# Two of four weight-block sums formed by accumulating DMAs, with the gate paired with minus the up projection

## The chip, the cores and the metric

The kernel runs on one core of one Trainium2 chip. The metric is the time of one execution on the device in microseconds (us); the time before is the median of three runs. The profile comes from one more execution, which the hardware profiler recorded.

## The reference

One decoder layer on a sequence of 512 tokens with 1024 channels, in float32. Around a token mixer (two attention branches) stand two SwiGLU blocks; the change is in these alone:

```
x = x + 0.5 * swiglu(rms_norm(x, ffn1_norm), w_gate, w_up, w_down)
...                                   # two attention branches, gated and merged
x = x + 0.5 * swiglu(rms_norm(x, ffn2_norm), w_gate, w_up, w_down)
out = rms_norm(x, final_norm)

swiglu(x) = (silu(x @ w_gate) * (x @ w_up)) @ w_down     # w_gate, w_up 1024 x 2816, w_down 2816 x 1024
```

## The kernel before, in words

All matrix products are made of three passes: each operand is split into a high part (a cast to float32r) and a low part (the rest), and low times high, high times high and high times low are summed in PSUM. A weight split is two instructions: `split` (L105) lets ScalarE (ACT) cast (L109) and VectorE (DVE) subtract (L110), into three rotating buffers `whi` and `wlo`.

The 2816 hidden columns of a SwiGLU are worked off in 11 pairs of 256 columns by `ffn_up` (L454). The first two pairs (`PLAIN`, L452) are plain products, and during the second of these the scaled activations `xhat` and the operands of the fast scheme are built: `Operands.early` (L372) forms the sums T3, T2 and T4 of activation blocks and splits them into `t3h`, `t3l` and so on, `Operands.late` (L385) splits the four blocks B11, T1, B21 and B22 over the plain operand's place. The other nine pairs go through `strassen_pair` (L389), a two-by-two block scheme with seven products instead of eight. One product (L397) is 24 matmuls of 128x128 weights by 256 tokens: gate and up, four blocks of rows, three passes. In the kernel before, the two block rows of the weights are the two halves of the pair's columns, for gate and up at once; the two block columns are the even and odd row blocks. The DVE forms four sums of weight blocks of 128x1024 elements per pair: `s1` (L418, for the product with T1), `s2` (L420, for T2), the difference of L429 (for T3) and that of L433 (for B22). The products run in this order: B11, T1, T2, B21, T3, B22, T4. The bank `a` collects B11, T2, T3 and T4; ACT copies it to SBUF in between (`keep`, L408), and the DVE adds these copies to the banks `c` and `b` (L428, L432, L435) into `C`. SiLU, the product of gate and up, and the split of the result (`hidden`, L337) end the pair.

After every second fast pair a down projection of the two pairs before it follows (`down1`, L537; `down2`, L1126). The weights of a pair (2 MB) come by two loads on SP's queue (`load_pair`, L445) into one of two large buffers, `raw` and `fraw`, which pairs and down projections take in turn. SP's loads wait there for a buffer.

In the first SwiGLU, before pairs 4 to 8, `rope_table` (L509) forms a table of sines: POOL's queue loads the positions (L515), DVE and ACT work on them, POOL's queue stores the table (L529). Later POOL builds the causal mask (L589, L590).

The order in which each engine and each queue takes its instructions is worked out when the program is built: the framework places each instruction by its place in the code and by a model of when its operands are ready, and puts in the semaphores. On the chip every engine and every queue then works in that fixed order. Only the very beginning (up to L311) is ordered by hand.

`sums` is a pool of two buffers with one tag, which the temporaries of `early` use first and then `s1` and `s2` of each pair.

Of the kernel before, what the change touches and what calls it, by code (L numbers as in the profile page):

```python
# [8 lines left out]
F32 = mybir.dt.float32  # L9
F32R = mybir.dt.float32r  # L10
I32 = mybir.dt.int32
AF = mybir.ActivationFunctionType
ALU = mybir.AluOpType
AX = mybir.AxisListType

P = 128
T = 512
NB = T // P
DM = 1024
KT = DM // P  # L20
# [36 lines left out]
def hybrid_layer_kernel(ctx: ExitStack, tc: tile.TileContext, x, positions,  # L57
# [6 lines left out]
    nc = tc.nc  # L64
    vec, act, pool, pe = nc.vector, nc.scalar, nc.gpsimd, nc.tensor
# [39 lines left out]
    def split(src, eng=None):  # L105
        shape = list(src.shape)
        hi = wspl.tile(shape, F32R, name="whi", tag="whi")
        lo = wspl.tile(shape, F32R, name="wlo", tag="wlo")
        act.copy(hi, src)  # L109
        (eng or vec).tensor_tensor(out=lo, in0=src, in1=as_f32(hi), op=ALU.subtract)  # L110
        return hi, lo

    def kview(w, c0, c1):
        return w[0].rearrange("(a p) n -> p a n", p=P)[:, :, c0:c1]
# [88 lines left out]
    ffn1_stack = ExitStack()  # L203
# [17 lines left out]
        vec.tensor_copy(Rb, ps)  # L221


    def ffn_pools(stack):
        names = (("work", 1), ("tt", 1), ("sums", 2))
        return [stack.enter_context(tc.tile_pool(name=n, bufs=b)) for n, b in names]

    raws.append(ffn1_stack.enter_context(tc.tile_pool(name="fraw", bufs=1)).tile([P, RAW], F32, name="fraw"))
    ffn1_pools = ffn_pools(ffn1_stack)

    with tc.tile_pool(name="xnat", bufs=1) as xnp:
        xn = xnp.tile([P, NB, DM], F32, name="xn")
# [13 lines left out]
        with tc.manual_schedule(engines={EN.PE, EN.Activation, EN.DVE}):  # L246
# [57 lines left out]
            for tb in range(NB):  # L304
# [3 lines left out]
                else:  # L308
                    vec.tensor_tensor_reduce(out=junk, in0=xn[:, tb, :], in1=xn[:, tb, :], scale=1.0, scalar=0.0,
                                             op0=ALU.mult, op1=ALU.add, accum_out=ssq[:, tb:tb + 1])  # L310
# [16 lines left out]
    HT = T // 2  # L327
# [3 lines left out]
    def bank8():  # L331
        return bank(next(turn8))

    def halves(ps):
        return ps.rearrange("p (g t) -> p g t", g=2)
# [22 lines left out]
    class Operands:  # L358
# [11 lines left out]
            vec.tensor_tensor(out=lo, in0=src, in1=as_f32(hi), op=ALU.subtract)  # L370

        def early(self):  # L372
            B, new = self.B, lambda nm: self.sums.tile([P, KT // 2, HT], F32, name=nm, tag="S")
            t3 = new("sum_t3")
            vec.tensor_tensor(out=t3, in0=B[1][1], in1=B[0][1], op=ALU.subtract)
            vec.tensor_tensor(out=B[0][1], in0=B[0][1], in1=B[0][0], op=ALU.subtract)
            self.put("T3", t3)
            t2 = new("sum_t2")
            vec.tensor_tensor(out=t2, in0=B[1][1], in1=B[0][1], op=ALU.subtract)
            self.put("T2", t2)  # L380
            t4 = new("sum_t4")
            vec.tensor_tensor(out=t4, in0=B[1][0], in1=t2, op=ALU.subtract)
            self.put("T4", t4)

        def late(self):  # L385
            for name, (i, j) in (("B11", (0, 0)), ("T1", (0, 1)), ("B21", (1, 0)), ("B22", (1, 1))):
                self.put(name, self.B[i][j])

    def strassen_pair(work, sums, ops, raw, G):  # L389

        A = [[raw[:, :, j::2, (1 - i) * P:(2 - i) * P] for j in range(2)] for i in range(2)]
        shape = [P, 2, KT // 2, P]

        def new(nm):
            return sums.tile(shape, F32, name=nm, tag="S")

        def product(ps, w, t, first):  # L397
            (wh, wl), (th, tl) = w, ops.t[t]
            for g in range(2):
                o = ps[:, g * HT:(g + 1) * HT]  # L400
                for k in range(KT // 2):
                    n = g == 0 and k == 0
                    last = g == 1 and k == KT // 2 - 1
                    pe.matmul(o, wl[:, g, k, :], th[:, k, :], start=first and n, stop=False, skip_group_check=True)  # L404
                    pe.matmul(o, wh[:, g, k, :], th[:, k, :], start=False, stop=False, skip_group_check=True)  # L405
                    pe.matmul(o, wh[:, g, k, :], tl[:, k, :], start=False, stop=last, skip_group_check=True)  # L406

        def keep(ps, nm):  # L408
            t = work.tile([P, T], F32, name=nm, tag="w", bufs=6)
            act.copy(t, ps)  # L410
            return t

        C = work.tile([P, 3, T], F32, name="C")
        a = bank8()
        product(a, split(A[0][0]), "B11", True)
        p1 = keep(a, "p1")
        s1 = new("s1")
        vec.tensor_tensor(out=s1, in0=A[1][0], in1=A[1][1], op=ALU.add)  # L418
        s2 = new("s2")
        vec.tensor_tensor(out=s2, in0=s1, in1=A[0][0], op=ALU.subtract)  # L420
        c = bank8()
        product(c, split(s1), "T1", True)
        p5 = keep(c, "p5")
        product(a, split(s2), "T2", False)
        u2 = keep(a, "u2")
        b = bank8()
        product(b, split(A[0][1]), "B21", True)
        vec.tensor_tensor(out=C[:, 1, :], in0=b, in1=p1, op=ALU.add)  # L428
        vec.tensor_tensor(out=A[1][0], in0=A[0][0], in1=A[1][0], op=ALU.subtract)  # L429
        product(a, split(A[1][0]), "T3", False)  # L430
        u3 = keep(a, "u3")
        vec.tensor_tensor(out=C[:, 0, :], in0=u3, in1=p5, op=ALU.add)  # L432
        vec.tensor_tensor(out=A[0][0], in0=A[0][1], in1=s2, op=ALU.subtract)  # L433
        product(c, split(A[0][0]), "B22", False)
        vec.tensor_tensor(out=C[:, 2, :], in0=c, in1=u2, op=ALU.add)  # L435
        product(a, split(A[1][1]), "T4", False)
        av = halves(a)
        act.activation(G[:, 1:4, :], C[:, :, 0:HT], AF.Silu)
        act.activation(G[:, 0, :], av[:, 0, :], AF.Silu)
        vec.scalar_tensor_tensor(out=G[:, 1:4, :], in0=G[:, 1:4, :], scalar=0.5, in1=C[:, :, HT:T],  # L440
                                 op0=ALU.mult, op1=ALU.mult)
        vec.scalar_tensor_tensor(out=G[:, 0, :], in0=G[:, 0, :], scalar=0.5, in1=av[:, 1, :],
                                 op0=ALU.mult, op1=ALU.mult)

    def load_pair(w_gate, w_up, m):  # L445
        raw = space(2 * KT, 2 * P).rearrange("p (g k) c -> p g k c", g=2)
        for g, w in enumerate((w_gate, w_up)):
            nc.sync.dma_start(out=raw[:, g], in_=kview(w, 2 * m * P, (2 * m + 2) * P))
        return raw

    NPAIR = FT // 2
    PLAIN = 2  # L452

    def ffn_up(pools, hp, w_gate, w_up, X, xsrc, xhat, gname, r, first, extra, down):  # L454
        work, ttp, sums = pools
        xg = x_parts(X)
        hs = {}
        ops = None
        for m in range(PLAIN):
            G = new_G(work)  # L460
            raw = None
            for s in range(2):
                f = 2 * m + s
# [7 lines left out]
                else:  # L471
                    if raw is None:
                        raw = load_pair(w_gate, w_up, m)
# [10 lines left out]
                if m == PLAIN - 1 and s == 0:  # L484
# [3 lines left out]
                    ops = Operands(ttp, sums, X, xhat)  # L488
# [3 lines left out]
        for m in range(PLAIN, NPAIR):  # L492
            if extra is not None:
                extra(m)
            G = new_G(work)
            strassen_pair(work, sums, ops, load_pair(w_gate, w_up, m), G)
            hs[m] = hidden(work, hp, G)
            if m % 2 == 0 and m + 2 < NPAIR:
                down([(n, hs.pop(n)) for n in (m - 2, m - 1)])
# [3 lines left out]
    rc = const.tile([P, 20], F32, name="rc")  # L503
    pool.dma_start(out=rc, in_=rope_const)
    tabd = [dram.tile([P, T], F32, name=f"tabd{j}") for j in range(5)]
    wk1, ttp1, sums1 = ffn1_pools


    def rope_table(m):  # L509
# [757 lines left out]
```

## Time and profile before

| what | value |
|---|---|
| median of the runs | 1098.73 us (1096.1 to 1101.28) |
| profiled execution | 1097.36 us |
| its span | 1095.4 us |
| mean granted clock of the TensorE | 0.995 |
| PE, DVE, ACT, POOL busy | 98%, 74%, 47%, 5% |
| moved by DMA | 132.90 MB, 121 GB/s on the mean |

The profile counts an engine as busy while an instruction runs on it. PE is the TensorE's matmul, PEld its weight load, which overlaps the matmuls. Times are counted from the start of the span. "x24" stands for 24 instructions; in an order of time, the brackets at the end of a row give the time for which the engine stood idle before and what ended that. Clock 1.00 is 2.4 GHz.

### The profile page before, as it was taken

Reading aid. Unit: us, or ns where it says so; the run is one execution under the profiler, and the core shown is the slowest. Engines: PE = TensorE matmul, PEld = TensorE weight load, DVE = VectorE, ACT = ScalarE, POOL = GpSimd, SP = SyncE. Lnnn points to the kernel's source line nnn. Section 1 sums busy time; section 2 is a strip of 40 time slices with the busy share of each in tenths; the row PEclk is TensorE's granted clock in tenths of the full one; section 3 lists DMA queues with packets and bytes.
Section 4 is the critical chain, followed back from the end, with each engine's and each line's share of the span. In section 5 each row is a group of like instructions: output and inputs, shape, how many; then the busy total and the mean of one; then the engine's idle time right before and its main releaser. Section 6 shows DMA issues by size and latency. Waiting matters only on the chain.

```text
span 1095.4 us, 15774 instructions
## 1 busy us (share of the span) xinstructions
PE 1072.3 (98%) x6268; PEld 936.7 (86%) x6268; DVE 815.4 (74%) x1331; ACT 513.8 (47%) x828; POOL 52.2 (5%) x53
## 2 busy tenths in 40 slices
PE   8979999999999999999999999999999999999997
PEld 6778999999898888788877777788889999898995
DVE  5978787988766767998478776659777766767753
ACT  6453544535254434676365543444434435253544
POOL 1020000000000100122000000000000000000003
PEclk9999999999999999999999999999999999999999
DMA  9205253334315315442756358412242314225211
GB/s 289 96 4 161 78 169 121 106 107 158 93 58 159 121 49 153 111 139 78 242 168 222 109 165 290 150 44 73 77 154 78 116 39 153 78 77 154 77 59 77
DMA packets 107033, 132.90 MB, mean 121 GB/s; under 512 B 4070, under 2 KB 87184, under 8 KB 106960
## 3 DMA queue, kind: packets, MB, share of 16 engines
q1 hardware_dynamic: 97392, 111.32, 32.1%
q10 hardware_dynamic: 7664, 15.18, 4.2%
q0 software_dynamic: 1904, 5.40, 1.7%
q8 instruction: 49, 0.80, 0.3%
q14 instruction: 24, 0.20, 0.1%
HBM read 114.32 MB, written 17.04 MB: 120 GB/s over the span
## 4 chain that ended last, share of the span: by engine, by line
PE 92%; DVE 4%; DMA 2%; ACT 1%; issue 1%; SPq 0%; DVEq 0%; ACTq 0%
PE bank_gb L117 9%; PE bank_gb L119 8%; PE bank_gb L118 8%; PE bank_sc L404 4%; PE bank_sc L405 4%; PE bank_sc L406 4%; PE bank_gb L404 3%; PE bank_gb L405 3%; PE bank_gb L406 3%; PE bank_tp L406 3%; PE bank_tp L405 3%; PE bank_sc L118 3%; PE bank_tp L404 3%; PE bank_sc L117 3%; PE bank_sc L119 3%; PE bank_tp L118 2%
## 5 line engine op out<-in xcount | busy, mean ns | idle before, releaser
L109 ACT CAST whi<-raw 128x1024 fp32r<-128x1024 f32 (+1 forms) x124 | 123.3, 996 | 120.2 <-PE bank_gb L119 31.1
L110 DVE TENSOR_TENSOR wlo<-raw,whi 128x1024 fp32r<-128x1024 f32 (+1 forms) x116 | 133.3, 1150 | 52.3 <-ACT whi L109 52.1
L110 DVE TENSOR_TENSOR wlo<-fraw,whi 128x1024 fp32r<-128x1024 f32 x77 | 92.1, 1197 | 48.8 <-ACT whi L109 48.7
L109 ACT CAST whi<-fraw 128x1024 fp32r<-128x1024 f32 x77 | 79.2, 1029 | 83.9 <-PE bank_gb L119 30.6
L117 PE MATMUL bank_gb<-xh,wlo 128*128 128x512 f32 x256 | 106.2, 415 | 0.0
L119 PE MATMUL bank_gb<-xl,whi 128*128 128x512 f32 x256 | 101.0, 395 | 0.0
L118 PE MATMUL bank_gb<-xh,whi 128*128 128x512 f32 x256 | 100.4, 392 | 0.0
L109 ACT CAST whi<-s 128x1024 fp32r<-128x1024 f32 x36 | 37.8, 1051 | 86.0 <-PE bank_sc L119 14.6
L404 PE MATMUL bank_sc<-xh,wlo 128*128 128x256 f32 x224 | 64.2, 287 | 5.0 <-DVE wlo L110 4.6
L405 PE MATMUL bank_sc<-xh,whi 128*128 128x256 f32 x224 | 64.1, 286 | 0.0
L406 PE MATMUL bank_sc<-xl,whi 128*128 128x256 f32 x224 | 64.1, 286 | 0.0
L117 PEld LDWEIGHTS bank_gb<-xh,wlo 128*128 128x128 f32 x256 | 48.4, 189 | 12.2 <-issue 3.0
L119 PEld LDWEIGHTS bank_gb<-xl,whi 128*128 128x128 f32 x256 | 48.2, 188 | 11.0 <-issue 0.4
L110 DVE TENSOR_TENSOR wlo<-s,whi 128x1024 fp32r<-128x1024 f32 x36 | 44.0, 1222 | 15.7 <-ACT whi L109 15.1
L118 PEld LDWEIGHTS bank_gb<-xh,whi 128*128 128x128 f32 x256 | 48.5, 190 | 8.0
L404 PEld LDWEIGHTS bank_sc<-xh,wlo 128*128 128x128 f32 x224 | 43.7, 195 | 5.6 <-issue 4.8
L783 DVE CUSTOM_DVE_ANT_0 bank_sc<-bank_sc,cmask 128x128 f32<-128x128 f32 (+3 forms) x64 | 31.5, 496 | 18.2 <-PE bank_sc L961 17.4
L405 PEld LDWEIGHTS bank_sc<-xh,whi 128*128 128x128 f32 x224 | 43.7, 195 | 0.1
L406 PEld LDWEIGHTS bank_sc<-xl,whi 128*128 128x128 f32 x224 | 43.8, 195 | 0.0
L406 PE MATMUL bank_gb<-xl,whi 128*128 128x256 f32 x144 | 41.0, 284 | 1.4 <-DVE xl L370 1.4
L404 PE MATMUL bank_gb<-xh,wlo 128*128 128x256 f32 x144 | 40.9, 284 | 0.5 <-ACT xh L369 0.5
L405 PE MATMUL bank_tp<-xh,whi 128*128 128x256 f32 x144 | 40.8, 283 | 0.0
(579 smaller groups left out, 3262.4 us busy)
## 6 DMA issues: line engine op xcount, KB each, us to landing
fraw<-in_ffn_w_up_dram SPq DMA_DIRECT2D x11, 1024.0 KB
fraw<-in_ffn_w_gate_dram SPq DMA_DIRECT2D x11, 1024.0 KB
raw<-in_w_in_dram SPq DMA_DIRECT2D x11, 1024.0 KB
raw<-in_ffn_w_up_dram SPq DMA_DIRECT2D x10, 1024.0 KB
raw<-in_ffn_w_gate_dram SPq DMA_DIRECT2D x10, 1024.0 KB
fraw<-in_ffn_w_down_dram SPq DMA_DIRECT2D x4, 2048.0 KB
raw<-in_ffn_w_down_dram SPq DMA_DIRECT2D x4, 2048.0 KB
raw<-in_w_in_dram SPq DMA_DIRECT2D x8, 512.0 KB
```

The costliest lines, as they stand in the source:

```text
L109: act.copy(hi, src)
L110: (eng or vec).tensor_tensor(out=lo, in0=src, in1=as_f32(hi), op=ALU.subtract)
L117: pe.matmul(ps, wl, xh, start=start, stop=False)
L118: pe.matmul(ps, wh, xh, start=False, stop=False)
L119: pe.matmul(ps, wh, xl, start=False, stop=stop)
L404: pe.matmul(o, wl[:, g, k, :], th[:, k, :], start=first and n, stop=False, skip_group_check=True)
L405: pe.matmul(o, wh[:, g, k, :], th[:, k, :], start=False, stop=False, skip_group_check=True)
L406: pe.matmul(o, wh[:, g, k, :], tl[:, k, :], start=False, stop=last, skip_group_check=True)
L783: vec.tensor_tensor_reduce(out=ps[:, 0:n], in0=ps[:, 0:n], in1=cmask[:, T - n:T], op0=ALU.add, op1=ALU.min, scale=-scale, scalar=3e38, acc ...
```

## The change

- The block rows of the fast scheme are now the gate (row 0) and minus the up projection (row 1), for all 256 columns of the pair; the block columns stay the even and the odd row blocks. The two halves of the columns take the place that gate and up had in a product.
- Two of the four sums of weight blocks come by DMA into a tile S: SP loads up's odd and gate's even row blocks, and accumulating DMAs on POOL's queue add up's even row blocks to each (`load_sums`). Both are kept as plain sums; the sign that this would need is put into the operands T2 and T4 and into a factor of -0.5 at the end.
- The other two sums stay on the DVE and are formed in the weight buffer's place.
- From pair 3 on, the B21 product is accumulated in PSUM on a copy of the B11 product (ACT copies from bank to bank) in place of a DVE addition behind it.
- SiLU runs in two pieces of 512 columns, the first one as soon as the B21 product is in. The tile `C` is gone.
- `sums` holds tiles of 8 KB per partition in place of 4 KB; T3 and T2 share one in `early`. In the first SwiGLU the pool `tt` is opened behind the start's tiles.

```diff
-    def ffn_pools(stack):
-        names = (("work", 1), ("tt", 1), ("sums", 2))
+    def ffn_pools(stack, names=(("work", 1), ("sums", 2), ("tt", 1))):
...
-    ffn1_pools = ffn_pools(ffn1_stack)
+    ffn1_pools = ffn_pools(ffn1_stack, (("work", 1), ("sums", 2)))
...
         def early(self):
-            B, new = self.B, lambda nm: self.sums.tile([P, KT // 2, HT], F32, name=nm, tag="S")
-            t3 = new("sum_t3")
+            B = self.B
+            t32, t4 = (self.sums.tile([P, 2, KT // 2, HT], F32, name=nm, tag="S") for nm in ("sum_t", "sum_t4"))
+            t3, t2, t4 = t32[:, 0], t32[:, 1], t4[:, 0]
             vec.tensor_tensor(out=t3, in0=B[1][1], in1=B[0][1], op=ALU.subtract)
-            vec.tensor_tensor(out=B[0][1], in0=B[0][1], in1=B[0][0], op=ALU.subtract)
+            vec.tensor_tensor(out=B[0][1], in0=B[0][0], in1=B[0][1], op=ALU.subtract)
             self.put("T3", t3)
-            t2 = new("sum_t2")
-            vec.tensor_tensor(out=t2, in0=B[1][1], in1=B[0][1], op=ALU.subtract)
+            vec.scalar_tensor_tensor(out=t2, in0=B[1][1], scalar=-1.0, in1=B[0][1], op0=ALU.mult, op1=ALU.subtract)
             self.put("T2", t2)
-            t4 = new("sum_t4")
-            vec.tensor_tensor(out=t4, in0=B[1][0], in1=t2, op=ALU.subtract)
+            vec.scalar_tensor_tensor(out=t4, in0=t2, scalar=-1.0, in1=B[1][0], op0=ALU.mult, op1=ALU.subtract)
             self.put("T4", t4)
...
-    def strassen_pair(work, sums, ops, raw, G):
+    def strassen_pair(work, ops, raw, S, G, seeded):
-        A = [[raw[:, :, j::2, (1 - i) * P:(2 - i) * P] for j in range(2)] for i in range(2)]
+        A = [[raw[:, i, j::2, :] for j in range(2)] for i in range(2)]
+        Gv = G.rearrange("p (f t) x -> p t f x", t=2)
...
-        a = bank8()
+        a, b, c = bank8(), bank8(), bank8()
         product(a, split(A[0][0]), "B11", True)
-        p1 = keep(a, "p1")
-        s1 = new("s1")
-        vec.tensor_tensor(out=s1, in0=A[1][0], in1=A[1][1], op=ALU.add)
-        s2 = new("s2")
-        vec.tensor_tensor(out=s2, in0=s1, in1=A[0][0], op=ALU.subtract)
-        c = bank8()
-        product(c, split(s1), "T1", True)
+        p1 = act.copy(b, a) if seeded else keep(a, "p1")
+        s2 = A[0][0]
+        vec.tensor_tensor(out=s2, in0=S[:, 0], in1=A[0][0], op=ALU.add)
+        product(c, split(S[:, 0]), "T1", True)
         p5 = keep(c, "p5")
         product(a, split(s2), "T2", False)
         u2 = keep(a, "u2")
-        b = bank8()
-        product(b, split(A[0][1]), "B21", True)
-        vec.tensor_tensor(out=C[:, 1, :], in0=b, in1=p1, op=ALU.add)
-        vec.tensor_tensor(out=A[1][0], in0=A[0][0], in1=A[1][0], op=ALU.subtract)
-        product(a, split(A[1][0]), "T3", False)
+        product(b, split(A[0][1]), "B21", not seeded)
+        if not seeded:
+            vec.tensor_tensor(out=p1, in0=b, in1=p1, op=ALU.add)
+        act.activation(Gv[:, 0], halves(b if seeded else p1), AF.Silu)
+        product(a, split(S[:, 1]), "T3", False)
         u3 = keep(a, "u3")
-        vec.tensor_tensor(out=C[:, 0, :], in0=u3, in1=p5, op=ALU.add)
-        vec.tensor_tensor(out=A[0][0], in0=A[0][1], in1=s2, op=ALU.subtract)
-        product(c, split(A[0][0]), "B22", False)
-        vec.tensor_tensor(out=C[:, 2, :], in0=c, in1=u2, op=ALU.add)
+        vec.tensor_tensor(out=p5, in0=u3, in1=p5, op=ALU.add)
+        vec.tensor_tensor(out=A[0][1], in0=A[0][1], in1=s2, op=ALU.add)
+        product(c, split(A[0][1]), "B22", False)
+        vec.tensor_tensor(out=u2, in0=c, in1=u2, op=ALU.add)
+        act.activation(Gv[:, 1], halves(u2), AF.Silu)
+        vec.scalar_tensor_tensor(out=Gv[:, 1], in0=Gv[:, 1], scalar=-0.5, in1=halves(p5), op0=ALU.mult, op1=ALU.mult)
         product(a, split(A[1][1]), "T4", False)
...
+        vec.scalar_tensor_tensor(out=Gv[:, 0], in0=Gv[:, 0], scalar=-0.5, in1=halves(a), op0=ALU.mult, op1=ALU.mult)
+
+    def load_sums(sums, w_gate, w_up, m):
+        S = sums.tile([P, 2, KT // 2, 2 * P], F32, name="S")
+        g, u = (kview(w, 2 * m * P, (2 * m + 2) * P) for w in (w_gate, w_up))
+        nc.sync.dma_start(out=S[:, 0], in_=u[:, 1::2])
+        nc.sync.dma_start(out=S[:, 1], in_=g[:, 0::2])
+        pool.dma_start(out=S[:, 0], in_=u[:, 0::2], accum_op=ALU.add)
+        pool.dma_start(out=S[:, 1], in_=u[:, 0::2], accum_op=ALU.add)
+        return S
...
-            strassen_pair(work, sums, ops, load_pair(w_gate, w_up, m), G)
+            raw = load_pair(w_gate, w_up, m)
+            strassen_pair(work, ops, raw, load_sums(sums, w_gate, w_up, m), G, m > PLAIN)
```

## Rows read from the trace of the kernel before

**Rows 1.** The page's first part: busy time, share of the span, instructions.

```profile
PE 1072.3 (98%) x6268; PEld 936.7 (86%) x6268; DVE 815.4 (74%) x1331; ACT 513.8 (47%) x828; POOL 52.2 (5%) x53
```

**Rows 2.** Busy time by stretch: its us; each engine's busy us; clock, DMA share, GB/s.

```profile
58.00:72.00 14.00, 7.98 (x49) 7.39 (x49) 13.75 (x13) 7.65 (x9) 6.51 (x2) 0.88 0.00 1
72.00:330.00 258.00, 258.00 (x1810) 242.94 (x1810) 203.93 (x240) 115.24 (x140) 5.61 (x11) 1.00 0.35 112
780.00:1060.00 280.00, 278.26 (x1927) 259.24 (x1926) 203.49 (x206) 125.69 (x150) 0.67 (x2) 1.00 0.29 96
```

**Rows 3.** PE's waits, the longest: us in total, times, longest.

```profile
PE bank_sc L404 <- DVE wlo L110: 4.6, 1, 4.6
```

**Rows 4.** PE in order of time, first fast pair, first SwiGLU: start, us, what.

```profile
62.75 0.28 PE L406 MATMUL bank_gb<-xl,whi 128*128 128x256 f32 x1
67.63 0.36 PE L404 MATMUL bank_sc<-xh,wlo 128*128 128x256 f32 x1 [4.61 <-DVE wlo L110]
...
72.07 0.28 PE L404 MATMUL bank_gb<-t2h,wlo 128*128 128x256 f32 x1
```

**Rows 5.** Busy time by stretch, behind PE's long wait.

```profile
67.70:72.00 4.30, 4.30 (x24) 4.30 (x25) 4.30 (x4) 0.74 (x1) 4.30 (x1) 0.60 0.00 0
72.00:84.00 12.00, 12.00 (x102) 12.00 (x102) 6.53 (x8) 5.88 (x8) 0.75 (x2) 1.00 0.20 60
```

**Rows 6.** Lines L418 and L429 on the DVE: ns min/median/max, first and last start.

```profile
L418 DVE TENSOR_TENSOR s<-raw x9: 1215/1224/1226, 56.6 to 996.0; 128x1024 f32<-128x1024 f32 x9
...
L429 DVE TENSOR_TENSOR raw<-raw x9: 1218/1218/1219, 67.4 to 998.4; 128x1024 f32<-128x1024 f32 x9
```

**Rows 7.** DVE in order of time, around the entry into the fast pairs.

```profile
53.68 1.22 DVE L370 TENSOR_TENSOR t2l<-sum_t,t2h 128x1024 fp32r<-128x1024 f32 x1
...
56.55 1.23 DVE L418 TENSOR_TENSOR s<-raw 128x1024 f32<-128x1024 f32 x1
...
65.13 1.22 DVE L420 TENSOR_TENSOR s<-s,raw 128x1024 f32<-128x1024 f32 x1
66.27 1.22 DVE L110 TENSOR_TENSOR wlo<-s,whi 128x1024 fp32r<-128x1024 f32 x1
```

**Rows 8.** SP's queue in order of time; then two stretches of 1 us.

```profile
46.92 0.37 SPq L102 DMA_DIRECT2D fraw<-in_ffn_w_down_dram  x1
...
48.00:49.00 1.00, 1.00 (x7) 0.81 (x6) 1.00 (x3) 0.47 (x1) 0.00 (x0) 1.00 0.51 115
...
53.00:54.00 1.00, 1.00 (x6) 0.81 (x6) 1.00 (x2) 0.19 (x1) 0.00 (x0) 1.00 0.87 356
```

**Rows 9.** DMA issues of POOL: times, KB each, median us to landing.

```profile
gfin<-in_final_norm_dram POOLq DMA_DIRECT2D x1, 512.0 KB, 3.8
...
pos<-in_positions_dram POOLq DMA_DIRECT2D x5, 256.0 KB, 4.8
```

**Rows 10.** The page's costliest groups: the two halves of a split.

```profile
L109 ACT CAST whi<-s 128x1024 fp32r<-128x1024 f32 x36 | 37.8, 1051 | 86.0 <-PE bank_sc L119 14.6
...
L110 DVE TENSOR_TENSOR wlo<-s,whi 128x1024 fp32r<-128x1024 f32 x36 | 44.0, 1222 | 15.7 <-ACT whi L109 15.1
```

**Rows 11.** DVE, then PE in order of time, entry of the second SwiGLU.

```profile
762.42 1.22 DVE L370 TENSOR_TENSOR t2l<-sum_t,t2h 128x1024 fp32r<-128x1024 f32 x1
...
782.80 0.39 PE L404 MATMUL bank_sc<-xh,wlo 128*128 128x256 f32 x1 [0.44 <-ACT xh L369]
...
789.90 0.36 PE L404 MATMUL bank_gb<-t2h,wlo 128*128 128x256 f32 x1 [0.84 <-DVE wlo L110]
```

**Rows 12.** POOL in order of time; then PE's T2 products in bank sc.

```profile
66.01 6.17 POOL L590 TENSOR_SCALAR_AFFINE_SELECT cmask<-cmask 128x128 f32<-128x128 f32 x1
82.51 0.57 POOL L515 DMA_DIRECT2D pos<-in_positions_dram  x1 [10.33 <-DVE C L432]
140.79 0.55 POOL L529 DMA_DIRECT2D tabd<-kk  x1 [57.71 <-DVE kk L528]
...
L404 PE MATMUL bank_sc<-t2h,wlo x48: 283/283/283, 134.2 to 897.5; 128*128 128x256 f32 x48
```

More of the change, by code (lines that the diff above doesn't have):

```diff
@@ L387, in late @@
                 self.put(name, self.B[i][j])
-    def strassen_pair(work, sums, ops, raw, G):
-        A = [[raw[:, :, j::2, (1 - i) * P:(2 - i) * P] for j in range(2)] for i in range(2)]
-        shape = [P, 2, KT // 2, P]
-        def new(nm):
-            return sums.tile(shape, F32, name=nm, tag="S")
+    def strassen_pair(work, ops, raw, S, G, seeded):
+        A = [[raw[:, i, j::2, :] for j in range(2)] for i in range(2)]
+        Gv = G.rearrange("p (f t) x -> p t f x", t=2)
         def product(ps, w, t, first):
             (wh, wl), (th, tl) = w, ops.t[t]
-            for g in range(2):
-                o = ps[:, g * HT:(g + 1) * HT]
+            for f in range(2):
+                o = ps[:, f * HT:(f + 1) * HT]
+                fs = slice(f * P, (f + 1) * P)
                 for k in range(KT // 2):
[L402 to L406, printed above, removed]
+                    n = f == 0 and k == 0
+                    last = f == 1 and k == KT // 2 - 1
+                    pe.matmul(o, wl[:, k, fs], th[:, k, :], start=first and n, stop=False, skip_group_check=True)
+                    pe.matmul(o, wh[:, k, fs], th[:, k, :], start=False, stop=False, skip_group_check=True)
+                    pe.matmul(o, wh[:, k, fs], tl[:, k, :], start=False, stop=last, skip_group_check=True)
         def keep(ps, nm):
@@ L411, in keep @@
             return t
-        C = work.tile([P, 3, T], F32, name="C")
-        a = bank8()
+        a, b, c = bank8(), bank8(), bank8()
         product(a, split(A[0][0]), "B11", True)
-        p1 = keep(a, "p1")
-        s1 = new("s1")
-        vec.tensor_tensor(out=s1, in0=A[1][0], in1=A[1][1], op=ALU.add)
-        s2 = new("s2")
-        vec.tensor_tensor(out=s2, in0=s1, in1=A[0][0], op=ALU.subtract)
-        c = bank8()
-        product(c, split(s1), "T1", True)
+        p1 = act.copy(b, a) if seeded else keep(a, "p1")
+        s2 = A[0][0]
+        vec.tensor_tensor(out=s2, in0=S[:, 0], in1=A[0][0], op=ALU.add)
+        product(c, split(S[:, 0]), "T1", True)
         p5 = keep(c, "p5")
@@ L435, in strassen_pair @@
-        vec.tensor_tensor(out=C[:, 2, :], in0=c, in1=u2, op=ALU.add)
-        product(a, split(A[1][1]), "T4", False)
[L437 to L443, printed above, removed]
+        product(b, split(A[0][1]), "B21", not seeded)
@@ L454, in ffn_up @@
     def ffn_up(pools, hp, w_gate, w_up, X, xsrc, xhat, gname, r, first, extra, down):
-        work, ttp, sums = pools
+        work, sums, ttp = pools
         xg = x_parts(X)
@@ L505, in hybrid_layer_kernel @@
     tabd = [dram.tile([P, T], F32, name=f"tabd{j}") for j in range(5)]
-    wk1, ttp1, sums1 = ffn1_pools
+    ffn1_pools += ffn_pools(ffn1_stack, (("tt", 1),))
+    wk1 = ffn1_pools[0]
     def rope_table(m):
```

## The prediction

> **What bounds the kernel now.** The page's first part comes first: the TensorE (PE) is busy in 98% of the span and VectorE (DVE) in 74% [rows 1]. A change that only takes work from the DVE can pay only where PE stands still for the DVE, so the next view is the busy time by stretch. In the first SwiGLU, from 72 us on, PE is busy in all 258.00 of 258 us, with the DVE busy 203.93 us beside it: the 2.4 us per pair that the change removes there lie under PE's work already. The second SwiGLU has 280 − 278.26 = 1.74 us of idle PE in all [rows 2]. What is left is the stretch from 58 to 72 us, the entry into the fast products: PE is busy 7.98 of 14 us, idle 6.02. PE's waits name the cause: the longest is 4.6 us for `wlo` of L110, the low half of a weight split [rows 3]. PE's order of time shows where: the first product's last matmul starts at 62.75, the second product (T1, on the sum of two weight blocks) at 67.63, the third at 72.07 [rows 4]. T1 thus took 4.44 us. In the next stretch 102 matmuls start in 12 us, 0.118 us each, so 24 of them want 2.8 us. The difference, 1.6 us, is the granted clock: 0.60 on average from 67.7 to 72 (part of the time at 1.2 GHz, after PE had stood idle), 1.00 afterwards [rows 5].
>
> So all that a faster DVE could give is 6.02 + 1.6 us at the first entry and 1.74 us at the second, 9.4 us or 0.9%. A difference of 0.5%, about 5.5 us, is what a measurement of this kernel can tell from none.
>
> **What the change does to the sums.** Per pair, two DVE instructions go, the sum of L418 (1224 ns) and the difference of L429 (1218 ns) [rows 6]: 18 pairs (nine on each weight buffer), 44 us of DVE time. Two stay (the in-place `s2` and the one before the B22 product). One add on the DVE (`C[:,1]`, L428) goes too where the second product starts on a copy of the first. That copy takes the place of the one to `p1` and costs ScalarE the same. PE's list is unchanged: seven products of 24 matmuls of the same shape. The three signs that turn are carried by instructions of the same kind and length, and the SiLUs are regrouped (2 x 512 columns in place of 768 + 256). All of this is priced at nothing: from 72 to 330 us the cover is PE's gapless work. Without that cover it would be a gain of 44 us and more, not a cost.
>
> Added per pair: two plain loads of 512 KB on SP's queue and two accumulating DMAs of 512 KB on POOL's, each behind the plain load of its half. SP's queue now has loads that wait for one of two buffers of S. The buffer is free once the pair two earlier has split its T3 block, and the weight load beside it waits for a later release, so nothing behind on SP is held back. On POOL the accumulating DMAs share an in-order queue with the rotary tables (the position load, the store of each table) and the mask.
>
> **The cost where it counts: first SwiGLU, first fast pair.** S for this pair reuses the buffer of `sum_t`, whose last reader before was t2l, starting at 53.68 and ending at 54.9 [rows 7]; `sum_t` holds T3 and T2 now, so that time stands. A plain load: the 2 MB issued at 46.92 move at 115 GB/s from 48 to 49 us and at 356 from 53 to 54 [rows 8]. So the data begin to flow some 1.3 us after issue, and 2 MB need about 6 us, 0.5 MB 1.5 us. With 0.4 us of issue the first half of S is in at 54.9 + 0.4 + 1.3 + 1.5 = 58.1. No row has an accumulating DMA. Nearest below: the 512 KB that POOL loads for `gfin` land 3.8 us after issue. Above: `pos`, 256 KB at 4.8 us, twice, 9.6 us, as if the read of the destination doubled the slowest POOL load [rows 9]. I take 5.5, nearer the load of the same size, because only the bytes at the SBUF end double. The Trainium skill ("DMA: Bandwidth & Descriptors", section "Anatomy of one DMA — SWDGE (gpsimd) path") fits such a DMA with 2.0 us plus its bytes at 436 GB/s, an estimate of 3.2 us for 512 KB; the rows' 3.8 us lie a little above it, and with 3.2 us the sum below would come out the same.
>
> The sum block is then in SBUF at 61.9 to 67.7, taken 63.6. Its split needs one ACT copy (1051 ns) and one DVE subtraction (1222 ns) [rows 10], about 2.4 us with the hand-over, so PE could start T1 at 64.3 to 70.1, taken 66.0. But the DVE has its own date. It works without a gap up to the split: `s` (L418) at 56.55, then the operand splits, `s2` at 65.13 and `wlo` at 66.27, which is PE's 67.63 [rows 7]. With L418 gone everything behind it moves 1.13 us ahead: 66.5. The later of both counts, 66.5, and the stall shrinks from 4.6 to 3.5 us: **−1.1 us**, with ends of −1.1 (DVE's date) and +2.5 (70.1 against 67.63). The low clock I leave as it is, because 3.5 us of idle PE remain; if the clock stayed up, 1.6 us more would go.
>
> **Second SwiGLU.** t2l starts at 762.42 there [rows 11], so S is in by about 764 + 8.7 = 773 (777 at the slow end), while PE first comes to T1 at 782.80. PE's longest wait there, 0.84 us before 789.90 [rows 11], is for the split that the T2 product needs. Behind the operand splits of this entry the DVE has neither of the two removed instructions (they ran in its slack before it), so the wait stays: 0, at best −0.8.
>
> **The other 16 pairs.** Each S has a buffer some 20 us or more before use (two pairs of seven products, 20 us each, share two buffers), and needs one plain load and one accumulation, 3.2 + 5.5 us, twice at the most: 0. A cycle of two pairs and a down projection holds four accumulations, which is 22 us of some 62 (the 258 us of rows 2 hold just over four cycles).
>
> **Sum.** −1.1 us. Against the profiled execution, 1097.36 us (span 1095.4 and 1.96 us around it), that gives 1096.3. The median of the runs, 1098.73, is 1.37 us above the profiled one, so as a median I say 1097.6; the times below are counted from that median too.
>
> **Rivals.**
> First, **the stall vanishes**: the order in which the instructions are issued is worked out anew, and if the DVE takes the split for the next product ahead of three of the instructions in front of it (two operand splits and `hl`, 1.13 us each), or PE takes the B21 product first, which needs no sum, PE restarts at 66.5 − 3.4 = 63.1, and the clock may stay up: −4.5 − 1.6 and −0.8 at the second entry, −6.9 us, 1091.8. For it: the orders of the queues are not those of the code (the mask of L590 ran ahead of the position load of L515 [rows 12]). Against: the splits in front stand earlier in the code, and B11 itself wants one of them.
> Second, ending **slower: POOL's order**. The mask's select runs 6.17 us on POOL, from 66.01 to 72.18, and starts once the operands of the first fast pair are split [rows 12]. If it is put ahead of that pair's accumulations, they start at 72.2, S is in at 77.7, PE starts T1 at 80.1: +12.5 us, 1111. It decides as soon as the accumulation is held past 66. Against it: the plain load lands at 58, before the mask can start.
> Third, also slower: an accumulation queued **behind a table's store**. POOL sits on the first store until 140.79; pair 4 has its T2 product at 134.2 [rows 12] and T1 24 matmuls before it, at 131.3. Queued behind, S is in at 141.3 + 5.5 and PE starts T1 at 149.2: +18 us, 1117. Against it: the buffer for pair 4 is free by PE's T3 product of pair 2, two products of 2.9 us after 72.07, so the load can be in some 55 us ahead of the store.
> Fourth, accumulation is far slower than any row: from 62/4 = 15.5 us for 512 KB the DMAs become the bound of both stages. At 20 us each cycle grows by 18 us, some 8 cycles 144 us, 1240. Nothing in the rows is within a factor of two of that.
> That the change doesn't do what it says would mean that PE had waited for the sums in most pairs, and rows 2 exclude it.
>
> **Chances.** Forecast 0.62, stall gone 0.17, mask first 0.12, behind a store 0.05, slow accumulation 0.04. The forecast has its own range of 1094 to 1102: −3.5 (with the clock kept and the 0.8 us) and +2.5, and 1 us more either way. The range of all, 1090 to 1111.5, takes in the first two rivals and leaves out the last two and the tails, under 0.2. Faster by over 0.5%: two thirds of the first rival and a little of the forecast (instructions ordered anew elsewhere), 0.16. Slower: the three slow rivals, 0.21, and a little of the forecast's end, 0.24. Within: 0.60.
>
> **What would show it.** In the new profile DVE's busy time falls by some 50 us and PE's stays. POOL's DMA issues grow by 36, the software queue's bytes by some 19 MB. PE's longest wait in this stretch is still T1's, for `wlo` of L110, near 3.5 us and ending near 66.5. If that wait ends at 80, or names a DMA, POOL's order or a slow accumulation decided; if it is gone, the first rival did. I am wrong if PE shows idle time between 72 and 330 us, or if accumulations take over 10 us.

## The result, and the profile after

The changed kernel takes 1137.12 us (median of four runs, 1133.42 to 1140.16) where the kernel before took 1098.16 (four runs beside it, 1096.10 to 1101.28): a ratio of 1.0354, 95% interval 1.0316 to 1.0392, **slower by 39 us**. The prediction was 1097.6 us within 1090 to 1111.5, so the size and the sign were wrong and the time lies outside the range. The profiled execution of the new kernel took 1133.42 us, the shortest of the four (span 1131.7, against 1095.4 before).

First the page's busy times, then busy time by stretch (us; busy us of PE, PEld, DVE, ACT, POOL; clock, DMA share, GB/s), both of the kernel after; they answer to [rows 1, 2]. The second SwiGLU comes some 36 us later there, so its last row is not the same work as in [rows 2]; from 816.3 to 1096.3, which is, PE is busy 276.82 us too.

```profile
PE 1081.1 (96%) x6268; PEld 946.0 (84%) x6268; DVE 765.3 (68%) x1279; ACT 511.9 (45%) x828; POOL 93.4 (8%) x89
```

```profile
58.00:72.00 14.00, 6.69 (x40) 6.24 (x40) 12.48 (x12) 7.43 (x9) 6.04 (x6) 0.81 1.19 245
72.00:330.00 258.00, 232.08 (x1515) 216.31 (x1515) 159.49 (x194) 95.53 (x116) 23.95 (x24) 0.94 0.60 162
139.20:147.00 7.80, 7.79 (x43) 7.79 (x44) 7.80 (x11) 4.04 (x5) 0.00 (x0) 0.61 0.01 2
...
290.70:300.00 9.30, 9.23 (x60) 9.23 (x61) 9.27 (x14) 5.18 (x7) 0.00 (x0) 0.75 0.01 2
263.00:270.00 7.00, 7.00 (x58) 7.00 (x59) 5.83 (x6) 3.56 (x6) 0.00 (x0) 1.00 0.00 0
780.00:1060.00 280.00, 276.82 (x1800) 252.97 (x1799) 185.48 (x192) 119.33 (x141) 23.32 (x18) 1.00 0.61 162
```

The DVE lost 50.1 us of work, as the change intends. PE gained nothing from it: the stretch from 72 to 330 us, which PE filled before, now has 25.92 us in which PE is idle. PE also looks busier by 8.8 us (1081.1 against 1072.3) with the same 6268 matmuls; 0.9 us of that lie before 58 us, where the change does nothing yet (54.31 against 53.45). The rest goes with the clock: from 139.20 on it was 0.61 and from 290.70 on 0.75, part of the time at 1.2 GHz, each time behind a stall of PE; from 263 on, behind a shorter one, it was 1.00. The 36.3 us by which the span grew are thus 27.5 us of idle PE (50.6 against 23.1 in the whole span) and 8.8 us of longer busy time.

PE's waits between 55 and 345 us, the longest three (us in total, times, longest), and then the rows of PE's order of time at which the entry's stall and three of the others end:

```profile
PE bank_sc L400 <- DVE wlo L110: 17.8, 3, 7.4
PE bank_gb L400 <- DVE wlo L110: 8.1, 2, 6.0
PE bank_tp L400 <- DVE wlo L110: 5.9, 1, 5.9
```

```profile
68.73 0.58 PE L400 MATMUL bank_tp<-xh,wlo 128*128 128x256 f32 x1 [5.90 <-DVE wlo L110]
...
139.21 0.58 PE L400 MATMUL bank_gb<-xh,wlo 128*128 128x256 f32 x1 [6.02 <-DVE wlo L110]
...
186.14 0.55 PE L400 MATMUL bank_gb<-xh,wlo 128*128 128x256 f32 x1 [2.10 <-DVE wlo L110]
...
290.77 0.58 PE L400 MATMUL bank_sc<-xh,wlo 128*128 128x256 f32 x1 [7.39 <-DVE wlo L110]
```

The last of the three waits is the entry's; it was 4.61 us before [rows 4]. The five others, 25.9 us, are new. Each stands ahead of the T1 product of one of the pairs 4 to 8 (6.02, 2.10, 7.06, 3.35 and 7.39 us), those in whose time the five rotary tables are formed. All name `wlo`, the split of the sum block S; but S itself had landed long before, and the DVE has more spare time than it had. So the question is what the split stands behind. The DVE's wait for the positions between 55 and 345 us, and its order of time around the first of the five stalls:

```profile
DVE ang L519 <- DMA pos<-in_positions_dram: 42.2, 5, 9.7
```

```profile
128.56 0.68 DVE L428 TENSOR_TENSOR u<-bank_tp,u 128x512 f32<-128x512 f32 x1
137.60 0.43 DVE L519 CAST ang<-pos 128x512 f32<-128x512 int32 x1 [8.35 <-DMA pos<-in_positions_dram]
137.94 1.22 DVE L110 TENSOR_TENSOR wlo<-S,whi 128x1024 fp32r<-128x1024 f32 x1
```

Before, this wait was 0.9 us in all, and the first cast ran at 125.55:

```profile
DVE ang L518 <- DMA pos<-in_positions_dram: 0.9, 2, 0.5
...
125.55 0.42 DVE L518 CAST ang<-pos 128x512 f32<-128x512 int32 x1
```

The cast needs the positions, and the DVE works in order: the split `wlo`, which PE wants, stands behind a cast that waits 8.35 us for a load. The stalls of pairs 6 and 8 read the same (the cast waits 9.38 and 9.72 us); these three are 20.5 of the 25.9 us.

In pairs 5 and 7 the same lateness comes by another way. There the cast waits under the down projection (6.83 us at 166.33), where PE has work, but the finished table is late too. Its store on POOL, and then what ACT does behind it:

```profile
177.87 0.55 POOL L530 DMA_DIRECT2D tabd<-kk  x1 [21.89 <-DVE kk L529]
```

```profile
183.34 0.33 ACTq L595 DMA_DIRECT2D table<-tabd  x1
183.78 1.05 ACT L109 CAST whi<-S 128x1024 fp32r<-128x1024 f32 x1 [5.84 <-DMA tabd<-kk]
```

The store is 13.8 us later than before (164.03). ACT loads the table back as soon as it is stored, and holds that load at the head of its own queue; the copy `whi` for T1's split stands behind it for 5.84 us, and PE stalls 2.10 us before 186.14. Why the position load is late stands in SP's and POOL's orders of time:

```profile
118.77 0.37 SPq L438 DMA_DIRECT2D S<-in_ffn_w_up_dram  x1
```

```profile
81.27 1.29 POOL L440 DMA_DIRECT2D S<-in_ffn_w_up_dram  x1 [14.80 <-DMA S<-in_ffn_w_up_dram]
83.91 1.28 POOL L441 DMA_DIRECT2D S<-in_ffn_w_up_dram  x1 [1.35 <-DMA S<-in_ffn_w_gate_dram]
123.18 1.28 POOL L440 DMA_DIRECT2D S<-in_ffn_w_up_dram  x1 [37.99 <-DMA S<-in_ffn_w_up_dram]
125.62 1.28 POOL L441 DMA_DIRECT2D S<-in_ffn_w_up_dram  x1 [1.17 <-DMA S<-in_ffn_w_gate_dram]
126.37 1.11 POOL L516 DMA_DIRECT2D pos<-in_positions_dram  x1
```

Read from the bottom: pair 4's position load was issued at 126.37, 44 us later than before (82.51 [rows 12]), because it stands directly behind the two accumulations of pair 5. The first of these held POOL for 37.99 us: it waits for its plain load, SP issues that at 118.77, and it could not earlier, because pair 5 takes the buffer of S that pair 3 had until its T3 split (on the DVE from 117.52 to 118.75). Once issued, the load also takes longer. The software queue (packets, MB, share of the DMA engines' time) and the DMA issues of POOL (KB each, median us from issue to landing) after:

```profile
q0 software_dynamic: 20912, 24.27, 11.8%
...
S<-in_ffn_w_up_dram POOLq DMA_DIRECT2D x36, 512.0 KB, 11.2
...
pos<-in_positions_dram POOLq DMA_DIRECT2D x5, 256.0 KB, 12.4
```

A position load lands 12.4 us after issue where it took 4.8 [rows 9], and an accumulation lands after 6.0 to 15.3 us, median 11.2. 126.37 and some 11 us make the cast's 137.60.

At the two entries S itself was late. The DVE's order of time at the first, and at the second; then ACT's and PE's at the second:

```profile
63.83 1.22 DVE L369 TENSOR_TENSOR xl<-xhat,xh 128x1024 fp32r<-128x1024 f32 x1
66.28 1.26 DVE L414 TENSOR_TENSOR raw<-S,raw 128x1024 f32<-128x1024 f32 x1 [1.24 <-DMA S<-in_ffn_w_up_dram]
67.47 1.21 DVE L110 TENSOR_TENSOR wlo<-S,whi 128x1024 fp32r<-128x1024 f32 x1
...
814.86 1.23 DVE L414 TENSOR_TENSOR fraw<-S,fraw 128x1024 f32<-128x1024 f32 x1 [6.63 <-DMA S<-in_ffn_w_up_dram]
```

```profile
814.87 1.05 ACT L109 CAST whi<-S 128x1024 fp32r<-128x1024 f32 x1 [8.16 <-DMA S<-in_ffn_w_up_dram]
...
818.34 0.39 PE L400 MATMUL bank_gb<-xh,wlo 128*128 128x256 f32 x1 [1.89 <-ACT xh L368]
```

The first costs PE 1.29 us more than before (5.90 against 4.61). At the second PE's longest wait is 1.89 us, against 0.84 [rows 11], and it isn't for S: the first product, B11, waits for an operand cast `xh`, which stands on ACT behind the copy of S. PE is idle 3.18 us in this stretch (280 − 276.82), against 1.74.

### The profile page after: what moved, and what is told of

It is laid out like the page before. It is cut to its first block, busy times and chain, and to the rows that moved or that the text cites. A ratio compares the mean times of both kernels' runs of the same rounds, so it can differ in the third digit from the quotient of the medians.

```text
span 1131.7 us, 15958 instructions
## 1 busy us (share of the span) xinstructions
PE 1081.1 (96%) x6268; PEld 946.0 (84%) x6268; DVE 765.3 (68%) x1279; ACT 511.9 (45%) x828; POOL 93.4 (8%) x89
## 3 DMA queue, kind: packets, MB, share of 16 engines
q0 software_dynamic: 20912, 24.27, 11.8%
## 4 chain that ended last, share of the span: by engine, by line
PE 75%; DMA 9%; DVE 7%; issue 6%; ACT 2%; POOL 1%; SPq 0%; ACTq 0%; POOLq 0%; DVEq 0%
PE bank_gb L117 8%; PE bank_gb L119 8%; PE bank_gb L118 8%; DMA S<-in_ffn_w_up_dram 4%; DMA pos<-in_positions_dram 3%; PE bank_tp L400 2%; PE bank_sc L400 2%; PE bank_gb L400 2%; PE bank_sc L401 2%; PE bank_sc L402 2%; PE bank_gb L402 2%; PE bank_tp L402 2%; PE bank_tp L401 2%; PE bank_gb L401 2%; DVE wlo L110 2%
## 5 line engine op out<-in xcount | busy, mean ns | idle before, releaser
L440 POOL DMA_DIRECT2D S<-in_ffn_w_up_dram x18 | 23.3, 1294 | 667.4 <-DMA S<-in_ffn_w_up_dram 355.7
L400 PE MATMUL bank_sc<-xh,wlo 128*128 128x256 f32 x208 | 61.3, 295 | 17.8 <-DVE wlo L110 17.8
L109 ACT CAST whi<-S 128x1024 fp32r<-128x1024 f32 x36 | 37.8, 1050 | 61.8 <-DMA S<-in_ffn_w_up_dram 12.5
L110 DVE TENSOR_TENSOR wlo<-S,whi 128x1024 fp32r<-128x1024 f32 x36 | 44.0, 1221 | 28.1 <-ACT whi L109 28.1
L401 PE MATMUL bank_sc<-xh,whi 128*128 128x256 f32 x208 | 60.8, 293 | 0.0
L402 PE MATMUL bank_sc<-xl,whi 128*128 128x256 f32 x208 | 60.7, 292 | 0.0
L117 PEld LDWEIGHTS bank_gb<-xh,wlo 128*128 128x128 f32 x256 | 48.1, 188 | 12.4 <-issue 3.0
L400 PE MATMUL bank_tp<-xh,wlo 128*128 128x256 f32 x160 | 46.5, 291 | 6.3 <-DVE wlo L110 5.9
L402 PE MATMUL bank_tp<-xl,whi 128*128 128x256 f32 x160 | 46.2, 289 | 0.0
L401 PE MATMUL bank_tp<-xh,whi 128*128 128x256 f32 x160 | 46.2, 289 | 0.0
## 6 DMA issues: line engine op xcount, KB each, us to landing
S<-in_ffn_w_up_dram POOLq DMA_DIRECT2D x36, 512.0 KB, 11.2
```

Of the source, the lines that this page charges most:

```text
L117: pe.matmul(ps, wl, xh, start=start, stop=False)
L400: pe.matmul(o, wl[:, k, fs], th[:, k, :], start=first and n, stop=False, skip_group_check=True)
L401: pe.matmul(o, wh[:, k, fs], th[:, k, :], start=False, stop=False, skip_group_check=True)
L402: pe.matmul(o, wh[:, k, fs], tl[:, k, :], start=False, stop=last, skip_group_check=True)
L440: pool.dma_start(out=S[:, 0], in_=u[:, 0::2], accum_op=ALU.add)
```

## The experiments

Theory A: POOL's in-order queue makes the position loads late. The rivals were that the accumulations' traffic alone does it (B), and that the new pairing, the copy in place of an addition and the SiLU order cost something by themselves (C). The diffs are against the kernel after unless said otherwise. The kernel before took, beside these runs, 1097.12 us (median of 30 runs, 1094.24 to 1100.49; of the 19 beside the first four kernels, the same 1097.12).

**Positions loaded once, at the start.** They leave POOL's queue in the SwiGLU; everything else of the change stays.

```diff
+        pos_i = xnp.tile([P, T], I32, name="pos_i")
+        pool.dma_start(out=pos_i, in_=positions[0].partition_broadcast(P))
+        pos = const.tile([P, T], mybir.dt.float16, name="pos")
...
+        vec.tensor_copy(pos, pos_i)
...
-        pos = wk1.tile([P, T], I32, name="pos", tag="w", bufs=6)
-        pool.dma_start(out=pos, in_=positions[0].partition_broadcast(P))
```

> The positions are loaded once at the start, kept as float16 (exact for these integers) and read from there for all five tables; everything else is as changed, accumulating DMAs included. Theory A (the five position loads stand behind accumulating DMAs on POOL's queue and on its ring, the DVE stands in its fixed order for them, and PE waits 25.9 us in five places and loses clock behind each): DVE's 42.2 us of waits for the positions and those five PE waits vanish, 1137 falls by about 33 to 1101 to 1107. Rival B (the accumulations' own traffic and lateness hold PE, the positions are only where it shows): PE still waits for weight splits between 100 and 330 us, and the time stays over 1120.

Measured: 1101.92 us, ratio to before 1.0047 (1.0030 to 1.0065). PE's busy time from 72 to 330 us:

```profile
72.00:330.00 258.00, 257.68 (x1791) 242.20 (x1790) 182.38 (x215) 114.77 (x137) 21.30 (x19) 0.99 0.62 166
```

PE fills the stretch again, though all 36 accumulations are there and are as slow as in the kernel after (median 11.1 us). So 35 of the 39 to 40 us hang on the position loads, and the accumulations' slowness by itself costs next to nothing in this stretch.

**The sums on the DVE, the rest of the change kept.**

```diff
+        vec.tensor_tensor(out=S[:, 0], in0=A[1][0], in1=A[1][1], op=ALU.add)
+        vec.tensor_tensor(out=S[:, 1], in0=A[0][0], in1=A[1][0], op=ALU.add)
...
     def load_sums(sums, w_gate, w_up, m):
         S = sums.tile([P, 2, KT // 2, 2 * P], F32, name="S")
+        return S
```

> The two sums are formed by the DVE into the same tile S, no DMA for S at all; the pairing of gate with minus up, the copy from bank to bank and the regrouped SiLU stay, and so do the position loads on POOL. Theory A: nothing stands before the position loads, so they land in about 5 us as before, and the time is within 6 us of the kernel before, 1093 to 1104. Rival C (the new pairing, the copy into the second bank or the order of the pieces costs time of its own): 1110 or more.

Measured: 1098.67 us, ratio 1.0016 (1.0002 to 1.0031). Pairing, copy and SiLU order cost 1.6 us by the medians (0.2 to 3.4 by the interval): C, which wanted 1110 or more, falls. A position load lands in 4.7 us here, as before.

**The POOL DMAs without their addition.** They overwrite S with up's even row blocks instead of adding them, so the sums of weight blocks are left out; queue, order, bytes from HBM and waits stay.

```diff
-        pool.dma_start(out=S[:, 0], in_=u[:, 0::2], accum_op=ALU.add)
-        pool.dma_start(out=S[:, 1], in_=u[:, 0::2], accum_op=ALU.add)
+        pool.dma_start(out=S[:, 0], in_=u[:, 0::2])
+        pool.dma_start(out=S[:, 1], in_=u[:, 0::2])
```

> The 36 DMAs on POOL's queue copy without adding (the sums are left out, S holds up's even row blocks alone); number, size, order and waits stay. If the addition is what makes them slow, their median landing falls from 11.2 us to 5 to 7 us, the positions land in 6 to 8 instead of 11 to 13.6, and the time falls to about 1108 to 1122. If the software queue or the plain loads beside them make them slow, landing stays at 10 or more and the time at 1130 or more.

Measured, in one run: 1112.69 us. Its software queue, POOL's DMA issues, and the DVE's wait for the positions:

```profile
q0 software_dynamic: 7088, 24.27, 6.4%
...
S<-in_ffn_w_up_dram POOLq DMA_DIRECT2D x36, 512.0 KB, 7.5
...
pos<-in_positions_dram POOLq DMA_DIRECT2D x5, 256.0 KB, 9.1
```

```profile
DVE ang L519 <- DMA pos<-in_positions_dram: 26.5, 5, 5.8
```

The addition is what makes these DMAs so slow (11.2 us to landing with it, 7.5 without), and it lengthens the DVE's waits from 26.5 to 42.2 us. But the same place in the queue without any addition still leaves 26.5 us of waits, and PE has 11.0 us of idle time from 72 to 330 us. So both count, the late issue and the slow landing. The time lies in the range expected for the addition as the cause, but both landings are slower than expected there (7.5 against 5 to 7, 9.1 against 6 to 8), so the addition isn't all that makes them slow.

**Positions loaded once, and the first fast pair's sums on the DVE.** That leaves 8 of 9 pairs of each SwiGLU with accumulating DMAs.

```diff
+        if not seeded:
+            vec.tensor_tensor(out=S[:, 0], in0=A[1][0], in1=A[1][1], op=ALU.add)
+            vec.tensor_tensor(out=S[:, 1], in0=A[0][0], in1=A[1][0], op=ALU.add)
...
+        if m == PLAIN:
+            return S
```

> Positions loaded once as in the run before of that name, and the two sums of the first fast pair of each SwiGLU on the DVE; the other 16 pairs keep their DMAs. Theory A with the entry as second cost (the accumulation lands late at both entries): another 3 to 6 us below the run with the positions alone, 1095 to 1102. Rival B: no change against that run, over 1120.

Measured: 1099.13 us, ratio 1.0018 (1.0007 to 1.0029). The late S at the two entries is worth 1101.92 − 1099.13 = 2.8 us (3 to 6 were expected). More is learnt from the stretch of the eight other pairs, here and with all sums on the DVE:

```profile
72.00:330.00 258.00, 257.85 (x1793) 242.39 (x1793) 180.93 (x214) 114.72 (x138) 21.08 (x19) 0.99 0.60 164
```

```profile
72.00:330.00 258.00, 257.74 (x1807) 242.51 (x1806) 196.63 (x231) 114.91 (x139) 5.41 (x10) 1.00 0.35 112
```

The DVE is busy 15.7 us less with the DMAs and PE is busy just as long. The times, 1099.13 and 1098.67 us, are the same within what the runs tell apart. With its two side effects taken away, forming the sums by DMA shows no gain. The two kernels differ in one more thing, where the positions are loaded; up to 58 us PE is busy alike in both (54.04 and 54.10 us), but a kernel with the positions loaded once and all sums on the DVE was not run.

**The position loads one pair earlier.** Still five, still on POOL's queue.

```diff
+    ahead = {}
+
+    def load_pos(m):
+        ahead[m] = wk1.tile([P, T], I32, name="pos", tag="w", bufs=6)
+        pool.dma_start(out=ahead[m], in_=positions[0].partition_broadcast(P))
+
     def rope_table(m):
         j = m - 4
+        if 0 <= j + 1 < 5:
+            load_pos(m + 1)
...
-        pos = wk1.tile([P, T], I32, name="pos", tag="w", bufs=6)
-        pool.dma_start(out=pos, in_=positions[0].partition_broadcast(P))
+        pos = ahead.pop(m)
```

> The kernel after, with each table's position load written one pair earlier (still on POOL's queue, still loaded for every table). Nothing is left out. Theory A (POOL's queue is in order, and a position load stands behind accumulations that wait for their S buffer): the loads stand two to four DMAs further ahead in POOL's order, the DVE's waits for pos between 55 and 345 us (42.2 us in five, in the kernel after) fall under 10 us, PE's five waits in pairs 4 to 8 (25.9 us) fall under 8 us, and the time is 1102 to 1112 us. Rival (the accumulations' traffic itself makes a position load slow, wherever it stands): landing from issue stays at 10 to 14 us and is still late, PE's five waits stay above 15 us, 1120 to 1137 us.

Measured: 1105.84 us, ratio 1.0057 (1.0031 to 1.0083). POOL's order of time, the landing of the loads, and PE's waits from 80 to 345 us, all of them:

```profile
86.25 1.29 POOL L441 DMA_DIRECT2D S<-in_ffn_w_up_dram  x1 [1.17 <-DMA S<-in_ffn_w_gate_dram]
87.01 1.11 POOL L514 DMA_DIRECT2D pos<-in_positions_dram  x1
125.74 1.28 POOL L440 DMA_DIRECT2D S<-in_ffn_w_up_dram  x1 [37.62 <-DMA S<-in_ffn_w_up_dram]
...
pos<-in_positions_dram POOLq DMA_DIRECT2D x5, 256.0 KB, 11.6
```

```profile
PE bank_pv L117 <- DVE wlo L110: 1.4, 1, 1.4
PE bank_sc L117 <- DVE wlo L110: 0.7, 1, 0.7
PE bank_sc L400 <- DVE wlo L110: 0.2, 1, 0.2
```

Pair 4's load now goes at 87.01, ahead of the accumulation that holds POOL until 125.74. It is nearly as slow as in the kernel after (11.6 us to landing), and harmless: the DVE has no wait for the positions left. That settles A against B: **the place in the queue decides, and the traffic only adds to it**. It gives back 31.3 us with not one byte less moved. Two of the five casts still wait, 3.82 and 4.54 us, now for a table's store, and the first two of PE's waits shown stand behind them.

By steps the 40.0 us between the kernel after (1137.12) and the one before (1097.12 in this series) are: position loads behind the accumulations 31.3 (to 1105.84), the position loads still in the queue 3.9 (to 1101.92), S late at the two entries 2.8 (to 1099.13), the rest 2.0. The kernel after was timed in an earlier series, beside a kernel before of 1098.16, so the first step may be 1 us smaller; and the steps below 4 us are near what the medians tell apart (the interval at 1105.84 alone is 2.9 us to either side).

**A version that beats both?** Before, the first entry ends on the DVE's own list, so in three kernels the low parts of three operands were worked out on POOL: in the kernel before, in the kernel of 1099.13 us (sums by DMA), and in the one of 1098.67 us (sums on the DVE). The same line in all three:

```diff
-            vec.tensor_tensor(out=lo, in0=src, in1=as_f32(hi), op=ALU.subtract)
+            (pool if name in ("T3", "T4", "B22") else vec).tensor_tensor(out=lo, in0=src, in1=as_f32(hi), op=ALU.subtract)
```

> The kernel before, with the low parts of the T3, T4 and B22 operands worked out on POOL in place of the DVE. Nothing is left out. PE's 4.6 us wait at the first entry ends on the DVE's own list; if three of the instructions in front of T1's split leave the DVE, PE starts T1 some 3 us earlier: 1092 to 1096 us. Rival (the POOL's instructions are slow, or contend with the DVE, and become the late ones): 1098 to 1106 us.

> The kernel after with the positions loaded once, the first fast pair's sums on the DVE, and the low parts of the T3, T4 and B22 operands worked out on POOL. Nothing is left out. On POOL the splits stand in order with the accumulating DMAs. If the accumulating DMAs can help anywhere it is here, with the DVE shortest: 1091 to 1096 us, at or below the kernel before with the same POOL splits. Rival (POOL's splits come to stand behind an accumulation that waits for its plain load, as the position loads did): PE waits for a split in the pairs behind, 1102 to 1130 us.

> The kernel after with all sums of weight blocks back on the DVE (no accumulating DMA) and the low parts of the T3, T4 and B22 operands worked out on POOL. Nothing is left out. Theory: the new pairing is worth nothing by itself, so this is the kernel before with POOL splits within 2 us, 1092 to 1097 us. Rival (the accumulating DMAs do bring something once POOL is used well): this is over 3 us slower than the one with them.

Measured: 1097.59 us, ratio 1.0003 (0.9990 to 1.0015); 1098.72, 1.0016 (1.0003 to 1.0029); 1098.37, 1.0006 (0.9993 to 1.0019). None is faster than the kernel before; all three came out above their forecasts and short of their rivals' times, though what the first one's rival names, POOL's instructions contending with the DVE's, is what its trace shows. In that run, POOL's order of time and then the DVE's:

```profile
56.48 2.40 POOL L370 TENSOR_TENSOR t4l<-sum_t,t4h 128x1024 fp32r<-128x1024 f32 x1 [3.99 <-ACT t4h L369]
66.12 3.17 POOL L370 TENSOR_TENSOR xl<-xhat,xh 128x1024 fp32r<-128x1024 f32 x1 [7.24 <-ACT xh L369]
```

```profile
55.24 1.21 DVE L370 TENSOR_TENSOR t2l<-sum_t,t2h 128x1024 fp32r<-128x1024 f32 x1
...
56.97 2.99 DVE L110 TENSOR_TENSOR wlo<-raw,whi 128x1024 fp32r<-128x1024 f32 x1
...
65.81 4.55 DVE L370 TENSOR_TENSOR xl<-xhat,xh 128x1024 fp32r<-128x1024 f32 x2
```

A subtraction that takes 1.21 us on the DVE alone took 2.99 beside POOL's, and it ended at 59.96, 1.08 us after POOL's had ended at 58.88. Two of them from 65.81 on took 4.55 us in place of 2.4, and ended at 70.36, 1.07 us after POOL's second (69.29). Both ends lie about one DVE subtraction behind POOL's, as if the DVE's began only then, so much of what was moved away came back as a block. In this execution (1100.03 us, the longest of its twelve) PE's 4.6 us wait is gone, but PE still reaches T2's product only at 72.88, where it was 72.07 before [rows 4].

## Why the prediction was wrong

**The step that failed is "The other 16 pairs … 0".** It asked whether S is in time for its own pair, and there it was right: none of the five new stalls is a wait for S to land. It did not ask what stands behind an accumulation on POOL. The text had the parts: it says that the accumulating DMAs "share an in-order queue with the rotary tables (the position load, the store of each table) and the mask". But it then priced an accumulation that comes late behind the mask or a store, and never the position load that comes late behind an accumulation. The trace of the kernel before would have given a bound. The load was issued at 82.51 [rows 12], landed 5.8 us later, and the cast that wants it ran at 125.55, so it could bear some 37 us of delay. It got 44 us, because the first accumulation of pair 5 held the queue for 37.99 us, and then landed 11.2 us after issue: the cast ran 12 us late.

Point by point:
- *PE gapless, so the DVE's freed time is worth nothing*: right for the freed time (257.85 against 257.74 us of busy PE in the pair of runs above), wrong as a cover for all of the change. PE was gapless only as long as the DVE's list had nothing late in it.
- *First entry −1.1 us, ends −1.1 and +2.5*: it came out at +1.3 on PE, inside the ends, with the wrong sign. The gain of 1.1 us wasn't there to be had. The text takes the DVE to work "without a gap up to the split"; it had one of 0.47 us behind L418, at an instruction that waits for PE. The DVE before, then after:

```profile
58.25 0.69 DVE L350 TENSOR_TENSOR u<-bank_sc,Rb 128x512 f32<-128x512 f32 x1 [0.47 <-PE bank_sc L119]
```

```profile
58.08 0.69 DVE L349 TENSOR_TENSOR u<-bank_sc,Rb 128x512 f32<-128x512 f32 x1 [1.60 <-PE bank_sc L119]
```

  With L418 gone the gap grew by those 1.13 us, and the DVE was free for `s2` at 65.05, before at 65.13 [rows 7]. S then came 1.24 us later still. Its plain load went at 54.77 (predicted 54.9) and was in by 59.49 (58.1), when the accumulation was issued; that landed 6.8 us later (5.5 was taken, 3.8 to 9.6 were the ends).
- *Second entry 0*: S came 6.6 us after the DVE was free for it, its accumulation 11.4 us after issue, and PE lost 1.4 us (3.18 against 1.74 us idle). The text asked whether S is there for T1; what came late was B11, for a cast that stands behind S's copy on ACT. The two entries together are the 2.8 us of the fourth experiment. The term that was mis-sized in both is the accumulation: over the kernel its median is 11.2 us, above the upper end of 9.6. The Trainium skill's fit ("DMA: Bandwidth & Descriptors", section "Anatomy of one DMA — SWDGE (gpsimd) path") gave an estimate of 3.2 us. The runs don't bear it out for accumulations: none in the kernel after came below 6.0, and even without the addition the median was 7.5.
- *Signs, copy, SiLU regrouped: 0*: right within 1.6 us by the medians (0.2 to 3.4 by the interval).
- *Rival 2, the mask ahead of the accumulations*: did not happen. The mask was set behind them, at 65.17, and its select took 0.29 us. So the 6.17 us [rows 12], on which this rival's price rests, isn't the select's own length; what held it before was not tried.
- *Rival 3, an accumulation behind a table's store*: the right queue, read the wrong way round.
- *Rival 4, slow accumulation as the bound of both stages*: the accumulations came near its 15.5 us (up to 15.3), but DMAs did not become the bound; the DMA share from 72 to 330 us is 0.60, and with the positions out of the way PE is gapless beside the same accumulations.
- *What would show it*: the DVE's 50 us, the 36 DMAs and the 19 MB (18.87) came as foretold; PE's busy time didn't stay (1081.1 against 1072.3). Both conditions named as "I am wrong if" came true, and the first, idle PE between 72 and 330 us, pointed to the place.

The 3.9 us between the loads one pair earlier and the loads taken away are explained only in part: in the profiles 2.0 us lie between 72 and 330 us (PE busy 255.67 against 257.68), and PE's two waits behind casts that wait for a table's store make up 2.1 us. How much of it is the queue and how much the traffic was not tried. Nor was a third buffer for S, which would let the plain loads start earlier.

## What to carry to other kernels

A DMA that waits for a buffer or for another DMA waits at the head of its issuing queue, and whatever stands behind it there, instructions of the engine too, waits along (here a position load behind 37.99 us of POOL's waiting, and a copy on ACT for 5.84 us). Before giving a queue such DMAs, list what else it issues, in order, with the time by which each is wanted; put loads that depend on nothing ahead of them, or on a queue without waits. A gapless engine hides work taken from another engine's list, but not a wait put into that list.

## What the runs showed of the hardware

- **An accumulating DMA costs far more than its bytes.** For the same 512 KB, the addition raised the packets of one DMA from 144 to 528 ((7088 − 1904) / 36 and (20912 − 1904) / 36; 1904 is the queue's count before), its issue on POOL from 0.75 to 1.28 us, and its median landing from 7.5 to 11.2 us.
- **POOL and the DVE do not run these subtractions side by side.** Each of the two slowed DVE rows above ended some 1.07 us after POOL's. The Trainium skill ("SBUF — State Buffer", section "SBUF: two separate sides") says that the two share a pair of ports as an exclusive lock, held for a whole instruction, when the DVE's operation has two inputs in SBUF and POOL's reads SBUF; both rows agree with it.
- **A stall can cost more than its length.** Behind the stalls of 6.02, 7.06 and 7.39 us the granted clock was 0.61 to 0.75 over the next 8 to 9 us, behind that of 2.10 us 0.57 over the next 4, and behind that of 3.35 us 1.00; over the kernel PE was busy 8.8 us longer (0.9 of them before 58 us), on top of 27.5 us of idle time. Why the one of 3.35 us went free was not tried.
